# Tying all TensorE work of the RWKV stage to the order of the source, in a one-core hybrid encoder step

## The chip, the cores and the metric

The kernel runs on one core of one Trainium2 chip. The core has five engines with an instruction stream each: TensorE (PE: matmuls and transposes), VectorE (DVE), ScalarE (ACT), GpSimd (POOL) and SyncE (SP, which issues the DMAs). Matmul results land in PSUM, an accumulator memory, from which VectorE and ScalarE read them. An engine takes its instructions in the order in which they stand in its stream; an instruction that needs another engine's result waits for a semaphore, and what stands behind it on its engine waits too. The metric is the device time of one execution in microseconds (us).

## The reference

One layer with three branches over 1,024 prompt positions and 64 sample positions, all from one projection of the normed input:

```python
z = rms_norm(h, prm['norm_g'][l]) @ prm['w_in'][l]
def step(S, inp):                       # branch A, RWKV-7, per head: S is 64 x 64
    r_t, w_t, k_t, v_t, kk_t, a_t = inp
    sa = jnp.einsum('bhij,bhj->bhi', S, -kk_t)
    S = (S * w_t[:, :, None, :] + sa[..., None] * (kk_t * a_t)[:, :, None, :]
         + v_t[..., None] * k_t[:, :, None, :])
    return S, jnp.einsum('bhij,bhj->bhi', S, r_t)
y_b = fox_attention(...)                # branch B: softmax(q.k/8 + c[t] - c[s]), causal
y_c = dsa_attention(...)                # branch C: top 256 keys by an indexer score, then softmax
h = h + gated @ prm['w_out'][l]
y = rms_norm(h, prm['final_g'])
```

## The kernel before

**Stages.** The kernel loads and norms the input, runs the indexer (branch C's scores), then the RWKV stage, then attention (branch B, then branch C) and the output. The projection of the input is split into pieces of 128 columns; `proj` (L154) makes a piece as 8 steps over the 1,024 input dimensions, each of three matmuls (`wb` with `uL`, `wh` with `uH`, `wl` with `uH`; called a k-step here) into a PSUM tile `pproj`. Finished pieces are parked in DRAM. They are *filling*: the pieces stand in a queue, and `pump` deals a few k-steps out behind every step of the other work.

**The RWKV stage** treats the sequence in units of four chunks of 64 positions, 16 units of the prompt and one of the sample. A unit passes through five streams, Python generators that stop at every `yield`: `prep` (`elem`, `chunk_rows`: decays, keys, masked products), `rows` (`value_rows`), `invert` (a 64 x 64 triangular inverse in five levels, the matmuls L1500, L1507 and L1514 in f16), `chain` (the recurrence) and `tail` (norm and gate). `braid` runs one step of them after the other in an interleaved order, with 0.7 k-steps of credit for `pump` behind each, while the top-k search of branch C (`topk`, VectorE and ScalarE only) runs on the side.

A step of the chain for one chunk `c` is: L1588 multiplies the state into PSUM, VectorE adds (L1589, `za`), L1593 multiplies, two VectorE copies make `UV` (L1598), and then, in one step of the source, L1601 makes the state's new part, VectorE turns it into the new state (L1606), and L1610 and L1612 make the output rows:

```python
        ch, ab = G(), self.gring("gd", 1)()
...
            for h in range(2):
                nc.tensor.matmul(ch[hv[h], c * 64:c * 64 + 64], BA[:, h, c, 64 * h:64 * h + 64], UV[:, h, c], start=True, stop=True)
...
            v.scalar_tensor_tensor(self.state, ch[:, c * 64:c * 64 + 64], Pt[:, c, 64:65], sp, op0=OP.mult, op1=OP.add)

            py = ch[:, 256 + c * 64:320 + c * 64]
            for h in range(2):
                nc.tensor.matmul(py[hv[1 - h]], BA[:, h, c, 64 - 64 * h:128 - 64 * h], UV[:, h, c], start=True, stop=False)
```

L1601 and L1610 write different columns of one PSUM tile, `ch` (`ps_gc` in the profile, 512 columns of four bytes), of which there is one buffer. `ps_ga` (the products of `prep` and `rows`) and `ps_tp` (transposes) have one buffer each too, `pproj` and `ps_gb` two.

**What sets the order.** The code is not emitted in the order in which it is written: a scheduler takes the instructions, simulates the engines, and places each where its engine can take it, by priority in the order of the source. Filling has its priority lowered by `LATE`, and `tied` forbids the first TensorE instruction of a filling step to pass TensorE's last instruction of the stream named in `self.now`. So main streams may pass filling and each other, and filling may slip back. One place has been in the order of the source before the change: the eight matmuls of L1442, by `in_order`. `rows_out` (L730) turns keys and values for the caches in three groups through the one `ps_tp` buffer, each group copied out by ScalarE before the next.

Of the kernel before, what the change touches and what calls it, by code (L numbers as in the profile page):

```python
# [85 lines left out]
class K:  # L86
# [77 lines left out]
    def tied(self, gen, engines):  # L164

        ins = self.nc.cur_bb.bb.instructions
        n = len(ins)
        self.tc.cur_priority += LATE
        more = next(gen, self) is not self
        self.tc.cur_priority -= LATE  # L170
        todo = set() if self.free else set(engines)
        for i in ins[n:]:
            if i.engine in todo:
                todo.discard(i.engine)
                for label, behind in self.behind.get(i.engine, {}).items():
                    if self.now and TIE2 and label != self.now:
                        continue
                    self.tc.add_manual_dep(i, behind, mybir.DependencyInfo(
                        mybir.DependencyClass.NoSync, mybir.DependencyReason.DATA), reason="order of issue")
        self.seen = len(ins)  # L180
        return more

    def note(self, label):

        ins = self.nc.cur_bb.bb.instructions
        for i in ins[self.seen:] if label in TIES or not TIES else ():
            self.behind.setdefault(i.engine, {})[label if TIE else 0] = i.name
        self.seen = len(ins)

    def in_order(self, n):  # L190

        last = None
        for i in self.nc.cur_bb.bb.instructions[n:]:
            if i.engine == PE:
                if last is not None:
                    self.tc.add_manual_dep(i, last, mybir.DependencyInfo(
                        mybir.DependencyClass.NoSync, mybir.DependencyReason.DATA), reason="order of issue")
                last = i.name

    def pump(self, n):  # L200

        self.credit = min(self.credit + n, 8)
        while self.credit >= 1 and self.fill:
            self.mark(self.fill[0][0])
            if self.tied(self.fill[0][1], (PE,)):
                self.credit -= 1
            else:
                self.filled.add(self.fill.popleft()[0])
# [1196 lines left out]
    @staticmethod  # L1405
    def dg(t, h):

        return t[64 * h:64 * h + 64, :, 64 * h:64 * h + 64]

    def chunk_rows(self, one, x):  # L1410

        nc = self.nc
        v, g, sc = nc.vector, nc.gpsimd, nc.scalar
        G = self.gring("ga", 1)
        QR, BK, ND = x["QR"], x["BK"], x["ND"]
        dg = self.dg

        BA = one.tile([P, 2, 4, 128], F32, tag="BA", name="BA", bufs=3)  # L1420
        BN = one.tile([P, 2, 4, 64], F32, tag="BN", name="BN", bufs=NBN)
        lo, hi = hv = (slice(0, 64), slice(64, 128))
        p1 = G()
        for c in range(4):
            self.turn(p1[:, c * P:c * P + P], BK[:, c, 0:2].rearrange("p a t -> p (a t)"))
        q1 = p1.rearrange("p (c h d) -> p c h d", h=2, d=64)
        sc.copy(BA[:, 0, :, 0:64], q1[:, :, 0])
        sc.copy(BA[hi, 1, :, 64:128], q1[lo, :, 1])
        sc.copy(BA[lo, 1, :, 64:128], q1[hi, :, 1])
        yield  # L1430
        am = self.con[:, C_AM:C_AM + P].rearrange("p (o x t) -> p o x t", o=1, x=2)
        ps = self.tp()
        nc.tensor.matmul(ps[:, :256], self.ones[:, C_BD - C_M:C_N - C_M], x["rk"], start=True, stop=True)
        x["vb"] = vb = one.tile([P, 4, 64], F32, tag="vb", name="vb", bufs=4)
        v.scalar_tensor_tensor(vb, ps[:, :256].rearrange("p (c t) -> p c t", t=64), 0.5, QR[:, :, 2], op0=OP.mult, op1=OP.mult)
        yield

        pm = G(), self.tp()
        at = len(nc.cur_bb.bb.instructions)
        for c in range(4):  # L1440
            for h in range(2):
                nc.tensor.matmul(pm[h][:, c * P:c * P + P], BK[hv[h], c, h:h + 2].rearrange("p a t -> p (a t)"),  # L1442
                                 QR[hv[h], c, 0:2].rearrange("p a t -> p (a t)"), start=True, stop=True)
        self.in_order(at)
        for h in range(2):
            q = pm[h].rearrange("p (c x t) -> p c x t", x=2, t=64)
            for i, dst in ((1, BN[:, h]), (0, BA[:, h, :, 64 - 64 * h:128 - 64 * h])):
                v.tensor_tensor(dst, q[:, :, i], am[:, :, i].broadcast_to([P, 4, 64]), op=OP.mult)
            g.tensor_scalar(dg(ND[:, 0], h), BN[hv[h], h], 1.0, 0.0, op0=OP.mult, op1=OP.add)
            g.tensor_tensor(dg(ND[:, 1], h), BN[hv[h], h], dg(ND[:, 0], h), op=OP.subtract)  # L1450
            if h == 0:
                yield
        x.update(BA=BA, BN=BN)
        yield
# [330 lines left out]
def program(ctx, tc, I, O):  # L1785
    s = K(ctx, tc, I, O)
# [25 lines left out]
    with ExitStack() as c2:  # L1812
        s.lr = s.pool("lr", ctx=c2, right=True)
        s.zs = s.pool("zs", bufs=1, ctx=c2, right=True)
        s.scp = s.pool("scp", ctx=c2, right=True)
        s.tkp = s.pool("tkp", ctx=c2, right=True)
        s.junk = s.pool("junk", ctx=c2, right=True)
        s.free = True
        s.weave(("idx", s.indexer()), R_IDX[0], R_IDX[1])
        ci.close()  # L1820
        s.rwkv_pools(c2)
        s.need("a0")
        s.free = False
        for nm, w, j in (("a2", s.park_a, 2), ("a3", s.park_a, 3), ("b0", s.park_b, 0),
                         ("b1", s.park_b, 1), ("b2", s.park_b, 2), ("b3", s.park_b, 3)):
            s.fill.append((nm, w(j)))
        for j in range(4):
            s.fill.append((f"c{j}", s.park_c(j)))
        for j in range(4):
            s.fill.append((f"g{j}", s.park_cg(j)))  # L1830
        units = [[(hp, 4 * q + i) for i in range(4)] for hp in range(4) for q in range(4)] + [[(hp, 16) for hp in range(4)]]
        topk = s.topk()
        n = len(units)
        x = [dict(ND=s.ND[u % 2]) for u in range(n)]
        s.weave(("prep0", s.prepare(units[0], x[0])), 10, R_A)
        for u in range(n + 2):
            work = []
            if u >= 2:
                work.append(("tail", s.tail(s.one, x[u - 2]), 3, ()))
            if 1 <= u <= n:  # L1840
                work.append(("chain", s.chain(s.one, units[u - 1], x[u - 1]), NCH, ()))
            if u < n:
                work.append(("invert", s.chunk_invert(s.one, x[u]), 14, ()))
                work.append(("rows", s.value_rows(s.one, x[u], u == n - 1), 2, ()))
            if u + 1 < n:
                if u % 4 == 3 and u < 15:
                    s.need(f"a{u // 4 + 1}")
                work.append(("prep", s.prepare(units[u + 1], x[u + 1]), 10, ()))
            if u < n:
                work.append(("topk", topk, N_TOPK, (DVE, ACT)))  # L1850
            work = [w[:3] for w in work if w[0] != "topk"]
            if u:
                next(s.bias, None)
            s.free = u >= FE
            s.braid(work, R_T if u > n else R_END if len(work) < 3 and u else R_A / 10, ("topk", topk, N_TOPK, (DVE, ACT), work[-1][0] if SIDE < 0 else work[SIDE][0]) if u < n else None)
        for _ in topk:
            pass
        s.need("b0")
        for _ in range(PX):
            s.pump(8)  # L1860
        if FX:
            s.free = False
# [83 lines left out]
```

## Time and profile before

| | |
|---|---|
| three runs, median (lowest to highest) | 1292.87 us (1289.9 to 1293.16) |
| profiled execution, its own time | 1289.49 us |
| its span, first to last instruction | 1286.6 us |
| PE busy, share of the span | 1230.5 us, 96% |
| DVE, ACT, POOL busy | 843.0, 780.3, 671.7 us |
| mean granted TensorE clock | 0.991 of full speed |

The span covers what the instructions take; some 2.9 us of the time lie around it. A matmul's end is modelled, so PE counts as busy up to the end of the last matmul's record, and a wait that starts before that shows shorter than it is. "PEld" is the loading of the stationary operand, which runs beside the matmuls.

### The profile page before, as it was taken

The numbers are of one execution on the slowest core, as the hardware profiler recorded it, in microseconds if no ns is written. First come the engines' busy times: TensorE is split into PE (matmuls) and PEld (weight loads), VectorE is DVE, ScalarE is ACT, GpSimd is POOL, SyncE is SP. The second block draws the span as 40 slices with busy tenths as digits, with TensorE's granted clock in tenths as the row PEclk, the third lists the DMA queues.
The fourth block names the chain that finished last, engine by engine and source line by source line (L and its number), as shares of the span: only waits on it lengthen the run. The fifth ranks groups of instructions, "written<-read, shape, count | busy, mean of one in ns | idle before, by whom it ended". The sixth has DMA issues, their size and how long they took to land.

```text
span 1286.6 us, 29362 instructions
## 1 busy us (share of the span) xinstructions
PE 1230.5 (96%) x10563; PEld 941.8 (73%) x10563; DVE 843.0 (66%) x2487; ACT 780.3 (61%) x1762; POOL 671.7 (52%) x973
## 2 busy tenths in 40 slices
PE   7999999999999999988999989999999889999997
PEld 5777777777777777666777767888887756777764
DVE  7468458888887787998564136556665588666642
ACT  7345357788877888544344456676664587655531
POOL 6333444545545655646454555576666477444311
PEclk9999999999999999989999999999999999999999
DMA  8332421232332443325225389676756476534323
GB/s 231 108 104 68 138 85 52 68 100 71 90 96 73 125 132 105 116 83 170 90 73 162 115 233 268 191 217 201 200 155 183 130 217 171 146 104 114 87 82 95
DMA packets 171699, 168.77 MB, mean 131 GB/s; under 512 B 38641, under 2 KB 146209, under 8 KB 171426
## 3 DMA queue, kind: packets, MB, share of 16 engines
q1 hardware_dynamic: 171554, 166.91, 44.7%
q8 instruction: 83, 1.36, 0.4%
q14 instruction: 62, 0.51, 0.1%
HBM read 106.18 MB, written 62.25 MB: 131 GB/s over the span
## 4 chain that ended last, share of the span: by engine, by line
PE 78%; DVE 9%; DMA 6%; ACT 3%; issue 2%; SPq 1%; POOL 0%; DVEq 0%; POOLq 0%; ACTq 0%
PE pproj L154 37%; PE pproj L1726 7%; PE ps_pv L1005 5%; PE ps_atp L107 4%; PE ps_tp L1726 4%; PE ps_sc L974 2%; PE ps_sc L975 2%; PE ps_gb L1500 2%; PE ps_tp L107 1%; PE ps_gb L1507 1%; ACT junka L613 1%; PE ps_gc L1610 1%; PE ps_gc L1612 1%; PE ps_gc L1601 1%; PE ps_ga L107 1%
## 5 line engine op out<-in xcount | busy, mean ns | idle before, releaser
L154 PE MATMUL pproj<-uH,wh 128*128 128x384 f32 (+4 forms) x1088 | 491.4, 452 | 0.0
L154 PE MATMUL pproj<-uH,wl 128*128 128x384 f32 (+4 forms) x1088 | 361.6, 332 | 0.0
L154 PE MATMUL pproj<-uL,wb 128*128 128x384 bf16 (+4 forms) x1088 | 356.9, 328 | 0.8 <-DVE shift L818 0.5
L154 PEld LDWEIGHTS pproj<-uH,wh 128*128 128x128 f32 (+1 forms) x1088 | 215.8, 198 | 4.8 <-issue 0.7
L154 PEld LDWEIGHTS pproj<-uH,wl 128*128 128x128 f32 (+1 forms) x1088 | 206.5, 190 | 2.0
L154 PEld LDWEIGHTS <-wb 128*128 128x128 bf16 (+1 forms) x1088 | 105.8, 97 | 116.5 <-issue 80.5
L613 ACT ACTIVATE junka<-score,tk_tau 128x1024 f16<-128x1024 f32 (+4 forms) x160 | 149.5, 934 | 33.1 <-DVE junk L607 22.1
L926 POOL TENSOR_SCALAR S<-S,mx 128x128 f32<-128x128 f32 (+8 forms) x136 | 105.6, 780 | 84.1 <-DVE mx L925 62.6
L140 POOL TENSOR_TENSOR wl<-wraw,wh 128x256 fp32r<-128x256 f32 (+1 forms) x184 | 137.8, 780 | 5.8 <-ACT wh L137 4.8
L943 ACT CAST hl<-ps_atp 128x512 fp32r<-128x512 f32 (+3 forms) x184 | 93.6, 515 | 76.8 <-PE ps_atp L107 67.1
L944 DVE TENSOR_TENSOR hl<-ps_atp,hl 128x512 fp32r<-128x512 f32 (+3 forms) x184 | 109.7, 600 | 45.1 <-ACT hl L943 43.4
L921 ACT ACTIVATE S<-S,mx 128x128 f32<-128x128 f32 (+8 forms) x136 | 105.8, 778 | 39.6 <-DVE mx L917 36.1
L142 POOL TENSOR_SCALAR wb<-wraw 128x512 bf16<-128x512 f32 (+1 forms) x92 | 62.9, 701 | 114.3 <-PE pproj L154 66.9
L1005 PE MATMUL ps_pv<-hl,VS 128*128 128x256 f32 (+3 forms) x640 | 111.9, 286 | 7.6 <-ACT hl L943 3.4
L1005 PEld LDWEIGHTS ps_pv<-hl,VS 128*128 128x128 f32 (+1 forms) x640 | 88.7, 173 | 20.7 <-DVE hl L944 4.7
L107 PE MATMUL ps_atp<-ident,S 128*128 128x128 f32 x616 | 101.7, 276 | 1.1 <-DVE hl L944 0.6
L1171 POOL TENSOR_TENSOR cb<-nm,T 128x256 f32<-128x256 bf16 (+2 forms) x80 | 54.3, 685 | 54.5 <-DVE mx L917 52.7
L107 PEld LDWEIGHTS ps_atp<-ident,S 128*128 128x128 f32 x616 | 74.8, 141 | 7.8 <-issue 1.0
L137 ACT CAST wh<-wraw 128x1024 fp32r<-128x1024 f32 (+1 forms) x46 | 47.7, 1037 | 35.9 <-PE pproj L154 35.4
L1726 PE MATMUL pproj<-oh,gh 128*128 128x512 f32 x144 | 67.4, 490 | 0.8 <-ACT oh L1705 0.5
L1726 PE MATMUL pproj<-ol,gb 128*128 128x512 bf16 (+1 forms) x144 | 52.4, 386 | 0.9 <-DVE ol L1706 0.9
L1598 DVE COPY UV<-ps_gd 64x64 f32<-64x64 f32 x136 | 29.9, 220 | 28.7 <-PE ps_gd L1593 26.5
(387 smaller groups left out, 2845.2 us busy)
## 6 DMA issues: line engine op xcount, KB each, us to landing
wraw<-in_w_in_dram SPq DMA_DIRECT2D x45, 512.0 KB
oraw<-in_w_out_dram SPq DMA_DIRECT2D x12, 512.0 KB
out_dram<-rows SPq DMA_DIRECT2D x10, 512.0 KB
x<-in_x_prompt_dram SPq DMA_DIRECT2D x8, 512.0 KB
wt<-a_wa SPq DMA_DIRECT2D x16, 256.0 KB
b_v<-vs SPq DMA_DIRECT2D x8, 512.0 KB
VS<-b_v SPq DMA_DIRECT2D x8, 512.0 KB
d_y<-y SPq DMA_DIRECT2D x64, 64.0 KB
```

The source lines that it names most:

```text
L107: self.nc.tensor.transpose(out, x, self.ident[:n, :n])
L140: nc.gpsimd.tensor_tensor(l[:, k:k + 2, :n], raw[:, k:k + 2, :n], h[:, k:k + 2, :n], op=OP.subtract)
L142: nc.gpsimd.tensor_scalar(b[:, k:k + 4, :n], raw[:, k:k + 4, :n], 1.0, 0.0, op0=OP.mult, op1=OP.add)
L154: self.nc.tensor.matmul(ps[:n, :nt], a[:, k, :n], b[:, k, t0:t0 + nt], start=(k == 0 and i == 0), stop=(k == KD - 1 and i == 2))
L613: nc.scalar.activation(junk[:, :sc.shape[1]], sc, AF.Sign, bias=tf[:, j:j + 1], accum_out=cnt[:, j:j + 1])
L921: nc.scalar.activation(S[:, :kn], S[:, :kn], AF.Exp, bias=mx[:, nm - 1:nm], scale=-1.0, accum_out=mx[:, 6:7])
L926: nc.gpsimd.tensor_scalar(S[:, :kn], S[:, :kn], mx[:, 7:8], 0.5, op0=OP.mult, op1=OP.mult)
L943: nc.scalar.copy(ph[:kr, a:b], ps[:kr, a:b])
L944: nc.vector.tensor_tensor(pl[:kr, a:b], ps[:kr, a:b], ph[:kr, a:b], op=OP.subtract)
L1005: nc.tensor.matmul(pv[0:m, q0:256], VS[:, kb, 0:m], hl[:, x, o:o + w], start=kb == 0 and x == 0, stop=at[-1][0] == last and n == 3)
L1171: nc.gpsimd.tensor_tensor(o, x, y, op=OP.add)
L1726: nc.tensor.matmul(ps[hf][:n, :], parts[m // 4][q][:, m % 4, :n], self.wo[m][q // 2][:, hf * 512:hf * 512 + 512], start=m == 0 and q == 0, ...
```

## The change

`strict` is a new attribute of the kernel. While it is not `None`, `tied` and `note` pass every TensorE instruction that has been emitted since the last call to `in_order`, which ties each to the one before it, and hand the last one's name on to the next call. The RWKV stage sets it from the first `prep` to the end of the loop over units. No instruction is added or taken away.

```diff
@@ tied @@
                     self.tc.add_manual_dep(i, behind, mybir.DependencyInfo(
                         mybir.DependencyClass.NoSync, mybir.DependencyReason.DATA), reason="order of issue")
+        if self.strict is not None:
+            self.strict = self.in_order(n, self.strict or None)
         self.seen = len(ins)
         return more
 
     def note(self, label):
 
         ins = self.nc.cur_bb.bb.instructions
+        if self.strict is not None:
+            self.strict = self.in_order(self.seen, self.strict or None)
...
-    def in_order(self, n):
-
-        last = None
+    strict = None
+
+    def in_order(self, n, last=None):
+
         for i in self.nc.cur_bb.bb.instructions[n:]:
             if i.engine == PE:
...
                 last = i.name
+        return last
@@ chunk_rows @@
-        self.in_order(at)
+        if self.strict is None:
+            self.in_order(at)
@@ program @@
+        s.strict = ""
         s.weave(("prep0", s.prepare(units[0], x[0])), 10, R_A)
         for u in range(n + 2):
...
+        s.strict = None
         for _ in topk:
             pass
```

In the changed kernel the lines of `chain` stand seven further down (L1601 is L1608 there, L1610 is L1617). On TensorE, one step of the chain stands like this before; `ps_gb` rows are the invert stream, `pproj` a k-step of filling, and the brackets name the engine whose semaphore an instruction waits for:

```order
L1601 MATMUL ps_gc<-UV,BA 64x64 [waits DVE_49] x2
L1507 LDWEIGHTS ND_1698
L1507 MATMUL ps_gb<-T_5485,ND_1698 128x64 [waits DVE_49]
...
L154 LDWEIGHTS wb
L154 MATMUL pproj<-uL,wb 128x384
L154 MATMUL pproj<-uH,wh 128x384
L154 MATMUL pproj<-uH,wl 128x384
L1610 MATMUL ps_gc<-UV,BA 64x64 [waits DVE_49]
L1610 MATMUL ps_gc<-UV,BA 64x64
L1612 MATMUL ps_gc<-S,QR 64x64 x2
```

The same step of the same unit on TensorE in the changed kernel:

```order
L154 LDWEIGHTS wb
L154 MATMUL pproj<-uL,wb 128x320
L154 MATMUL pproj<-uH,wh 128x320
L154 MATMUL pproj<-uH,wl 128x320
L1608 MATMUL ps_gc<-UV,BA 64x64 [waits DVE_49] x2
L1617 MATMUL ps_gc<-UV,BA 64x64 [waits DVE_49]
L1617 MATMUL ps_gc<-UV,BA 64x64
L1619 MATMUL ps_gc<-S,QR 64x64 x2
L1507 LDWEIGHTS Y_5668
```

The level of the inverse and the k-step that stood between the two products of the chain now stand elsewhere, and the second product follows the first at once.

The second place is `rows_out` for a piece of keys, on TensorE before; `kT` is the piece, `ps_tp` the one buffer that ScalarE empties between the groups:

```order
L154 MATMUL pproj<-uH,wl 128x320
L107 MATMUL ps_tp<-ident,kT 128x128 x4
L1500 LDWEIGHTS U_6536
L1500 MATMUL ps_gb<-Y_6556,U_6536 64x64 [waits DVE_49]
...
L1601 MATMUL ps_gc<-UV,BA 64x64 [waits DVE_49] x2
L107 MATMUL ps_tp<-ident,kT 128x128 [waits Activation_49]
L107 MATMUL ps_tp<-ident,kT 128x128 x3
```

And the same piece in the changed kernel:

```order
L1595 MATMUL ps_gd<-S,QR 64x64 x2
L107 MATMUL ps_tp<-ident,kT 128x128 x4
L107 MATMUL ps_tp<-ident,kT 128x128 [waits Activation_49]
L107 MATMUL ps_tp<-ident,kT 128x128 x3
L107 MATMUL ps_tp<-ident,kT 64x128 [waits Activation_49]
L154 LDWEIGHTS wb
```

The three groups of transposes, between which other matmuls stood, now stand one behind the other.

## Rows read from the trace of the kernel before

**Rows 1.** The page: span, and busy time by engine
```profile
span 1286.6 us, 29362 instructions
...
PE 1230.5 (96%) x10563; PEld 941.8 (73%) x10563; DVE 843.0 (66%) x2487; ACT 780.3 (61%) x1762; POOL 671.7 (52%) x973
```

**Rows 2.** The page: chain of work that ended last, shares by engine
```profile
PE 78%; DVE 9%; DMA 6%; ACT 3%; issue 2%; SPq 1%; POOL 0%; DVEq 0%; POOLq 0%; ACTq 0%
```

**Rows 3.** Three windows of the RWKV stage: length, busy (x instructions) by engine, clock
```profile
166.00:500.00 334.00, 326.27 (x3969) 247.03 (x3968) 262.27 (x850) 267.07 (x610) 181.22 (x282) 1.00 0.31 93
500.00:605.00 105.00, 93.88 (x1052) 70.35 (x1051) 92.08 (x259) 52.89 (x127) 59.21 (x82) 0.97 0.37 114
605.00:720.00 115.00, 112.82 (x1289) 82.97 (x1290) 58.40 (x180) 45.12 (x114) 56.61 (x88) 1.00 0.31 97
sum 554.00, PE 532.97 PEld 400.34 DVE 412.74 ACT 365.08 POOL 297.04; mean PE 177.66 PEld 133.45 DVE 137.58 ACT 121.69 POOL 99.01
```

**Rows 4.** Waits of PE, 166 to 720 us: total us, times, longest
```profile
PE ps_gc L1610 <- DVE S L1606: 2.3, 6, 0.6
PE ps_ga L107 <- DVE BK L1393: 2.2, 2, 1.1
PE ps_gb L1500 <- DVE Y L1538: 1.9, 6, 0.5
PE ps_gb L1507 <- DVE T L1543: 1.6, 4, 0.6
```

**Rows 5.** Timeline, 301 to 303 us: start, length, instruction
```profile
301.08 0.33 PE L154 MATMUL pproj<-uL,wb 128*128 128x384 bf16 x1
...
301.42 0.34 PE L154 MATMUL pproj<-uH,wl 128*128 128x384 f32 x1
...
301.60 0.34 PE L154 MATMUL pproj<-uL,wb 128*128 128x384 bf16 x1
...
301.95 0.34 PE L154 MATMUL pproj<-uH,wl 128*128 128x384 f32 x1
...
302.21 0.34 PE L1610 MATMUL ps_gc<-UV,BA 128*64 128x64 f32 x4
...
302.60 0.23 PE L1588 MATMUL ps_gd<-S,QR 64*64 64x64 f32 x2
...
302.76 0.34 PE L154 MATMUL pproj<-uL,wb 128*128 128x384 bf16 x1
```

**Rows 6.** Timeline, 419.7 to 421 us
```profile
419.76 0.34 PE L1601 MATMUL ps_gc<-UV,BA 128*64 128x64 f32 x4
...
420.02 0.66 PE L107 MATMUL ps_tp<-ident,kT 128*128 128x128 f32 x4
...
420.61 0.31 PE L1500 MATMUL ps_gb<-Y,U 64*64 64x64 f16 x8
...
420.71 0.59 ACT L730 COPY rows<-ps_tp 128x512 f32<-128x512 f32 x1 [0.43 <-PE ps_tp L107]
```

**Rows 7.** Timeline, 433.9 to 434.9 us; in brackets the idle time before
```profile
433.94 0.34 PE L1601 MATMUL ps_gc<-UV,BA 128*64 128x64 f32 x4
...
434.35 0.28 DVE L1606 SCALAR_TENSOR_TENSOR S<-ps_gc,Pt,sp 128x64 f32<-128x64 f32 x1
...
434.69 0.34 PE L1610 MATMUL ps_gc<-UV,BA 128*64 128x64 f32 x4 [0.41 <-DVE S L1606]
```

**Rows 8.** Line L1606: its instructions, and what DVE sat idle for before them
```profile
L1606 DVE SCALAR_TENSOR_TENSOR S<-ps_gc,Pt,sp x64: 265/280/286, 206.7 to 690.5; 128x64 f32<-128x64 f32 x64
...
L1606 DVE SCALAR_TENSOR_TENSOR s_end<-ps_gc,Pt,sp x4: 283/284/284, 701.1 to 719.1; 128x64 f32<-128x64 f32 x4
...
  PE ps_gc L1601: 20.0, 22
```

**Rows 9.** DVE groups by form, 166 to 720 us: busy, mean ns, idle before
```profile
L607 DVE TENSOR_SCALAR_CACHE_REDUCE junk<-scores,tk_tau 64x576 f16<-64x576 f32 x32 | 25.6, 798 | 4.4 <-ACT junka L613 4.4
```

**Rows 10.** Timeline, 300 to 302 us: the reads of `ps_ga` after L1354
```profile
300.17 0.50 PE L1354 MATMUL ps_ga<-ones,k 128*128 128x2 f32 x4
...
300.53 0.60 PE L107 MATMUL ps_tp<-ident,Yt 128*64 128x128 f32 x4
...
300.70 0.47 ACT L1356 ACTIVATE lw<-ps_ga,par 128x256 f32<-128x256 f32 x1 [0.96 <-PE ps_ga L1354]
...
301.80 0.15 DVE L1359 TENSOR_SCALAR ass<-ps_ga 128x4 f32<-128x4 f32 x1
```

**Rows 11.** Windows around the drop of the clock (the column of 0.72)
```profile
540.00:550.00 10.00, 6.92 (x71) 4.99 (x71) 9.91 (x18) 4.36 (x9) 9.70 (x9) 1.00 0.28 90
550.00:560.00 10.00, 7.90 (x76) 6.13 (x76) 8.74 (x23) 2.79 (x7) 3.30 (x9) 0.72 0.44 151
580.00:595.00 15.00, 11.38 (x135) 8.69 (x133) 14.80 (x38) 8.11 (x23) 12.02 (x20) 1.00 0.68 211
```

**Rows 12.** Timeline of PE, 551 to 553 us
```profile
551.52 0.50 PE L154 MATMUL pproj<-uL,wb 128*128 128x384 bf16 x1
...
552.46 0.54 PE L154 MATMUL pproj<-uL,wb 128*128 128x384 bf16 x1
```

## The prediction, made before the changed kernel had run

> **What bounds the kernel now.** I read the page first. TensorE is busy for 1230.5 of 1286.6 us [rows 1], and 78% of the chain of work that ended last lies on it [rows 2]: what TensorE loses anywhere, the kernel loses, unless it was waiting there already. Next the windows of the stage that the change reorders, from 166 us (the first product of `prep`) to 720 us (the last product of the chain). TensorE is busy for 532.97 of 554.00 us there, so all its idle time is 21.0 us [rows 3]: 7.7 us up to 500, 11.1 us from 500 to 605, where DVE is busy for 92.08 of 105 us and is nearly the bound itself, and 2.2 us after. The list of waits splits this into many small ones: six of L1610 for the state, two of L107 for `BK`, six of L1500 and four of L1507 for the levels of the inverse [rows 4]. So the most that any order of this stage could win is 21 us, 1.6% of the time; there is no such limit on what one can lose.
>
> **What the change moves.** The changed order holds the same instructions. From the first product of `prep` to the first score of attention I count 5,547 matmuls in both orders, 1,917 of them filling; ahead of that stretch and behind it TensorE's orders are the same. Inside it, filling stood in 276 runs and now stands in 455, nearly always one k-step at a time. Four terms follow.
>
> *Changes of hands.* From a k-step's last matmul to the next k-step it is 0.18 us (301.42 to 301.60); a recurrence product follows a k-step's last matmul after 0.26 us (301.95 to 302.21), and a k-step follows a recurrence product after 0.16 us (302.60 to 302.76) [rows 5]. 179 more runs mean 179 x (0.26 + 0.16) = 75 us; against it stand 213 fewer borders between two k-steps (38 us) and 276 fewer between two recurrence groups (44 us at 0.16). That is -7 us at the outside and nothing to the accuracy of these borders; I take 0. The matmuls themselves cost what they did.
>
> *The state in the chain.* This is the term that decides. L1601 and L1610 are one step of the source, and in the changed order L1610 stands right behind L1601 in all 68 steps of the chain (16 units of four chunks and the sample's four), where before this was so in three, and elsewhere a level of the inverse, k-steps or transposes stood between. L1610 waits for DVE, and by the trace for L1606, which reads the new state's product out of the same PSUM tile. One of the three shows the price: L1601 starts at 433.94, L1606 runs from 434.35 to 434.63, L1610 starts at 434.69 [rows 7], 0.75 us after L1601, though DVE was free. Where something else follows L1601, it starts 0.26 us behind (419.76 to 420.02) [rows 6]. So each new neighbour costs 0.49 us, and 65 of them 32 us. That is for a free DVE. In 22 of its 68 runs L1606 found DVE idle and waiting for it [rows 8]; in the other 46 something was ahead in DVE's queue. Bounds for that: nothing at all below, and above a whole top-k count of 0.80 us [rows 9] each time, 37 us. A DVE instruction of the first window takes 262.27 / 850 = 0.31 us on average [rows 3]; it is nearest to the usual case, and 46 x 0.31 = 14 us is what I take. The term: 46 us, from 32 to 69. Queued behind L1610 on TensorE is all its work, so nothing covers the wait.
>
> Why L1610 waits at all, when it writes other columns than L1606 reads, no row says. [...]
>
> *Transposes through one buffer.* `rows_out` runs seven times inside the tied stretch, and its three groups now stand together, so that two of them wait for ScalarE's copy: 14 waits. A group starts at 420.02, the next matmul follows at 420.61, but the copy of `ps_tp` ends at 420.71 + 0.59 = 421.30 [rows 6], and with the 0.06 us that L1610 took after L1606's end [rows 7] the next group could start at 421.36: 0.75 us each, 10.5 us. The copy is not sooner than its input, so this is the lower end; another ScalarE instruction of 0.47 us [rows 10] ahead of it each time would make 17 us.
>
> *`ps_ga`.* `prep`'s first product (L1354) and `rows`' transposes (L107 of `QR`) use the same single buffer, and now stand one k-step apart. L1354 started at 300.17, its last reader L1359 ended at 301.80 + 0.15 = 301.95 [rows 10]; between the two there will be L1354's own 0.36 us (to 300.53) and a k-step's 0.52, so the transposes wait 1.78 + 0.06 - 0.88 = 0.96 us as it was here, or 0.33 us if L1359 follows L1356 (300.70 + 0.47) at once. With 16 such pairs 5 to 15 us; I take the middle, 10 us.
>
> *What the old waits give back.* Between the inverse's products there is now a k-step or a chain product almost everywhere, so the waits of L1500 and L1507 should largely go; those from 500 to 605 us come from DVE, which isn't relieved. I take half of the 21.0 us, 10.5 us; the bounds are all and none.
>
> The sum is 46 + 10.5 + 10 - 10.5 = 56 us. On the profiled execution's own 1289.49 us that is 1345.5 us; that execution was 3.4 us under the median of the three runs shown, 1292.87, which makes 1349 us, and I say 1348 because waits that come at the same moment count once. Low end: 32 + 10.5 + 5 - 21 = 26.5 us, 1319 us. High end: 69 + 17 + 15 - 0 = 101 us, 1394 us; all terms at their worst together are unlikely, and the range ends at 1386 us.
>
> **The rivals.** *DVE's queue in full (chance 0.11).* If L1606 stands behind a top-k count in all 46 cases, and `ps_ga`'s reader too, the time is 1394 us. For it: DVE is busy for 79% up to 500 us and 88% from 500 to 605 [rows 3]. Against: while TensorE waits, DVE catches up.
>
> *The clock (0.05).* At 551 us the granted clock fell to half: a k-step took 0.94 us (551.52 to 552.46) [rows 12] instead of 0.52, after ten microseconds in which TensorE was busy for 6.92 [rows 11]. The clock column of 550 to 560 is 0.72, so 5.6 of the ten ran at half speed; a k-step loses 0.42 of its 0.94 us there, so such a stretch costs some 2.5 us. If the new waits bring on one in each of the 17 units, the time is 43 us longer than forecast, 1391 us. Against: from 580 to 595 us TensorE was busy for 11.38 of 15 us and kept the full clock [rows 11], and the forecast leaves it busy for 533 of 610, 87%. [...]
>
> *Faster (0.03).* If L1606 were done in time everywhere, the fixed order would show only its good side: all 21.0 us of waits gone, 1272 us. It decides where more than 0.49 us of other work stands between L1601 and L1610; the order shows none. The same comes about if the old waits were caused by the scheduler's misjudged times, and the new ones are shorter than a free DVE needs, which [rows 7] speaks against.
>
> *No change that shows (0.03), within 0.3%, which is about what a measurement of this kernel can tell from none.* The losses would have to be covered because DVE is the true bound. That holds from 500 to 605 us at most, and by its share of the stage's time 13 of the 68 chain steps lie there: 6 of the 32 us.
>
> My forecast has 0.78. The range of 1319 to 1386 us holds it and the nearer half of the first two rivals. Slower by over 0.3%: 0.78 + 0.11 + 0.05 = 0.94; within 0.3%: 0.03; faster: 0.03.
>
> **What would show it.** In the list of TensorE's waits, `ps_gc` L1617 (L1610 before) for the state of L1613 (L1606) should come first, some 68 times, with 20 to 40 us shown (part of each wait lies under the modelled end of L1608). L107 should wait some 14 times for the copy of `rows` (L736 there) and some 15 times for `ass` (L1365). L1608 to L1617 should take 0.75 us or more from start to start. TensorE's idle time between the same two products should grow from 21 to 60 or 90 us, and attention should take as long as before. I am wrong if L1617 waits for less than 0.2 us a time, if waits of the inverse take the place of those that I count as gone, or if the clock column of the stage falls under 0.95.

## The result and the profile after

| | before | after |
|---|---|---|
| median of four runs (lowest to highest) | 1293.01 us (1289.9 to 1293.91) | 1411.37 us (1408.96 to 1413.29) |
| profiled execution, its own time | 1289.5 us | 1413.2 us |

The ratio is 1.0928, 95% interval 1.0901 to 1.0955: slower by 118 us, where 56 were forecast. The time lies outside the range. The two profiled executions differ by 123.7 us, and the accounts below go by these.

The page of the changed kernel (first row span, then busy time, then the granted clock in 40 slices, then the chain that ended last):

```profile
span 1411.4 us, 29349 instructions
...
PE 1281.9 (91%) x10563; PEld 968.2 (69%) x10563; DVE 844.4 (60%) x2487; ACT 786.4 (56%) x1762; POOL 668.4 (47%) x973
...
PEclk9999989999899999989999999999999989999999
...
PE 70%; DVE 12%; ACT 6%; DMA 6%; issue 3%; POOL 2%; SPq 1%; DVEq 0%; POOLq 0%; ACTq 0%
```

DVE, ACT and POOL are busy for as long as before [rows 1], TensorE for 51 us more, though it has the same 10,563 matmuls. So TensorE did not only wait: its matmuls took longer, or started further apart.

Windows of the reordered stage, with the columns of [rows 3]; the fourth is the whole of it, from the first product of `prep` (146.9 us, not the 166 that the prediction names; before it was 146.1) to the first score of attention (869.8, before 750.1), and the last row is the whole stage before the change:

```profile
166.00:500.00 334.00, 293.27 (x3252) 215.29 (x3250) 219.14 (x712) 227.87 (x509) 140.00 (x224) 0.95 0.23 70
500.00:605.00 105.00, 89.16 (x980) 64.51 (x980) 69.03 (x224) 63.54 (x144) 46.86 (x76) 0.93 0.34 105
605.00:720.00 115.00, 91.59 (x975) 66.35 (x976) 78.91 (x204) 40.11 (x99) 55.15 (x78) 0.93 0.28 88
...
146.00:870.00 724.00, 628.73 (x6626) 459.12 (x6625) 422.22 (x1312) 391.82 (x894) 321.07 (x499) 0.95 0.29 88
...
146.00:750.00 604.00, 582.31 (x6620) 437.14 (x6618) 423.56 (x1312) 386.23 (x894) 327.86 (x499) 0.99 0.34 104
```

TensorE is busy for 628.73 of 724 us, 87%, the share that was forecast. The column to look at is the clock: 1.00, 0.97 and 1.00 before, 0.95, 0.93 and 0.93 now.

TensorE's waits in that stage (total, times, longest):

```profile
PE ps_gc L1617 <- DVE S L1613: 48.8, 64, 2.2
PE ps_tp L107 <- ACT rows L736: 15.4, 14, 2.2
PE ps_ga L107 <- DVE ass L1365: 10.0, 16, 2.0
PE ps_gc L1608 <- DVE UV L1605: 3.4, 1, 3.4
PE ps_gb L1514 <- DVE T L1550: 2.9, 6, 1.2
...
PE ps_gc L1617 <- DVE s_end L1613: 1.9, 4, 0.5
```

The three waits that were forecast are the three largest, in the places and as often as forecast: 68, 14 and 16 times. Together they are 76.1 us of the 95.2 us that TensorE stands idle between the two products named (21.4 before).

One of the 68 at work, on TensorE and then on VectorE:

```profile
299.85 0.34 PE L1608 MATMUL ps_gc<-UV,BA 128*64 128x64 f32 x4
302.04 0.34 PE L1617 MATMUL ps_gc<-UV,BA 128*64 128x64 f32 x4 [1.86 <-DVE S L1613]
```

```profile
300.13 0.41 DVE L1455 TENSOR_TENSOR BA<-ps_ga,con 128x256 f32<-128x256 f32 x1
300.46 0.15 DVE L823 COPY shift<-pproj 128x1 f32<-128x1 f32 x1
300.52 0.41 DVE L1455 TENSOR_TENSOR BN<-ps_tp,con 128x256 f32<-128x256 f32 x1
300.86 0.41 DVE L1455 TENSOR_TENSOR BA<-ps_tp,con 128x256 f32<-128x256 f32 x1
301.19 0.15 DVE L824 COPY shift<-pproj 128x1 f32<-128x1 f32 x1
...
301.38 0.41 DVE L1545 TENSOR_TENSOR Y<-ps_gb,con 128x256 f16<-128x256 f32 x1
301.72 0.27 DVE L1613 SCALAR_TENSOR_TENSOR S<-ps_gc,Pt,sp 128x64 f32<-128x64 f32 x1
```

L1613 needs what L1608 wrote by 300.2, but six instructions of other streams (and two more, left out here) stand ahead of it in VectorE's queue. L1617 starts 0.05 us after L1613's end, 2.19 us after L1608. And now the clock (windows of two microseconds, the same columns):

```profile
301.00:303.00 2.00, 0.96 (x19) 0.78 (x19) 1.50 (x9) 1.63 (x5) 1.52 (x3) 1.00 0.71 282
303.00:305.00 2.00, 2.00 (x12) 1.29 (x10) 0.85 (x4) 1.24 (x2) 1.35 (x2) 0.67 0.03 8
305.00:307.00 2.00, 2.00 (x15) 1.57 (x15) 1.06 (x4) 1.11 (x3) 0.00 (x0) 0.50 0.00 0
```

TensorE was idle for half of 301 to 303; from 303.7 on it runs at half of the full clock (0.50 from 305 to 307), while it is busy all the time. The granted clock falls 15 times in the stage and is at half speed for 71.7 us in all by the clock records (before: twice, 6.8 us). This fall is like the others: in the five microseconds ahead of each of the 15, TensorE stood idle for 1.3 to 3.1 us, where five microseconds of the stage hold 0.7 us of idle time on average. Other stretches with as much idle time kept the full clock (from 665 to 670 TensorE was idle for 2.04 us, and the clock column is 1.00 there and up to 675).

One thing more changed, which no list of waits shows. Before, the chain's last product (L1612) and the next chunk's first (L1588) mostly started within 0.01 us of each other, so that the two took little longer than one (the fourth row of these, at 302.60, and the k-step behind it, at 302.76, stand in [rows 5]):

```profile
302.48 0.27 PE L1612 MATMUL ps_gc<-S,QR 64*64 64x64 f32 x2
302.49 0.27 PE L1588 MATMUL ps_gd<-S,QR 64*64 64x64 f32 x2
302.59 0.22 PE L1612 MATMUL ps_gc<-S,QR 64*64 64x64 f32 x2
```

In the changed kernel a k-step follows the last product (L1619) in 50 of 68 steps, and L1619 alone takes as long, 0.26 us to the next start, as the two together before, 0.28 us:

```profile
224.38 0.33 PE L1619 MATMUL ps_gc<-S,QR 64*64 64x64 f32 x4
224.64 0.34 PE L154 MATMUL pproj<-uL,wb 128*128 128x384 bf16 x1
```

### The profile page after: what moved, and what is told of

Same layout as the page of the kernel before. It is cut to its first block, busy times and chain, and to the rows that moved or that the text cites. A ratio compares the mean times of both kernels' runs of the same rounds, so it can differ in the third digit from the quotient of the medians.

```text
span 1411.4 us, 29349 instructions
## 1 busy us (share of the span) xinstructions
PE 1281.9 (91%) x10563; PEld 968.2 (69%) x10563; DVE 844.4 (60%) x2487; ACT 786.4 (56%) x1762; POOL 668.4 (47%) x973
## 4 chain that ended last, share of the span: by engine, by line
PE 70%; DVE 12%; ACT 6%; DMA 6%; issue 3%; POOL 2%; SPq 1%; DVEq 0%; POOLq 0%; ACTq 0%
PE pproj L154 32%; PE pproj L1733 7%; PE ps_pv L1011 4%; PE ps_atp L107 4%; PE ps_tp L1733 4%; ACT junka L619 2%; PE ps_sc L980 2%; PE ps_sc L981 2%; PE ps_gb L1507 2%; DVE junk L613 1%; PE ps_gc L1617 1%; PE ps_tp L107 1%; DVE S L1613 1%; PE ps_gc L1619 1%; PE ps_gd L1595 1%
## 5 line engine op out<-in xcount | busy, mean ns | idle before, releaser
L154 PE MATMUL pproj<-uH,wh 128*128 128x384 f32 (+4 forms) x1088 | 503.7, 463 | 0.0
L154 PE MATMUL pproj<-uH,wl 128*128 128x384 f32 (+4 forms) x1088 | 366.1, 336 | 0.0
L154 PE MATMUL pproj<-uL,wb 128*128 128x384 bf16 (+4 forms) x1088 | 363.3, 334 | 0.5 <-DVE shift L824 0.5
L154 PEld LDWEIGHTS pproj<-uH,wh 128*128 128x128 f32 (+1 forms) x1088 | 220.5, 203 | 5.1
L154 PEld LDWEIGHTS pproj<-uH,wl 128*128 128x128 f32 (+1 forms) x1088 | 212.2, 195 | 1.4
L142 POOL TENSOR_SCALAR wb<-wraw 128x512 bf16<-128x512 f32 (+1 forms) x92 | 59.4, 664 | 120.3 <-issue 63.1
L1617 PE MATMUL ps_gc<-UV,BA 128*64 128x64 f32 x272 | 23.2, 250 | 50.6 <-DVE S L1613 48.8
L1456 POOL TENSOR_SCALAR ND<-BN 64x256 f16<-64x256 f32 x34 | 13.7, 402 | 113.3 <-DVE BN L1455 112.1
```

The lines of the kernel that those rows point to most:

```text
L142: nc.gpsimd.tensor_scalar(b[:, k:k + 4, :n], raw[:, k:k + 4, :n], 1.0, 0.0, op0=OP.mult, op1=OP.add)
L154: self.nc.tensor.matmul(ps[:n, :nt], a[:, k, :n], b[:, k, t0:t0 + nt], start=(k == 0 and i == 0), stop=(k == KD - 1 and i == 2))
```

## The experiments

All are compared with before. *Stage* is the time from the first product of `prep` (L1316 of before) to the first score of attention, *idle* the sum of TensorE's shown idle times in it, *half* the time at which the granted clock was 0.5 in it; all come from the profiled executions. *Left over* is the stage less before's 604.0, less the idle time above 21.4, less 0.45 us for each us of half above 6.8; 0.45 is (0.94 - 0.52) / 0.94, from [rows 12] and the prediction's full-speed k-step. Each ratio is against runs of the kernel before that were taken with it, whose medians are 1290.3 to 1293.0 us. The executions of one kernel differ in their clock: e1's profiled one, the slowest of its four (1353.7 us), was granted 0.971 and the other three 0.980 to 0.982, and in e3, e5, e6 and e7 too the profiled one had the lowest clock. *Half* is therefore on the high side in these rows.

| kernel | median us | ratio, 95% | stage | idle | half | left over | behind the stage |
|---|---|---|---|---|---|---|---|
| before | 1293.0 | | 604.0 | 21.4 | 6.8 | 0 | 536.5 |
| after | 1411.4 | 1.0928 [1.0901, 1.0955] | 723.0 | 95.2 | 71.7 | 16.0 | 541.6 |
| e1_banks | 1347.5 | 1.0457 [1.0431, 1.0483] | 665.3 | 56.2 | 54.6 | 5.0 | 540.3 |
| e2_before_banks | 1304.2 | 1.0114 [1.0096, 1.0132] | 615.4 | 28.4 | 17.1 | -0.2 | 540.3 |
| e3_dummy | 1398.6 | 1.0847 [1.0822, 1.0873] | 711.5 | 51.8 | 47.8 | more work | 540.0 |
| e4_banks_rows | 1339.5 | 1.0387 [1.0367, 1.0406] | 654.2 | 50.4 | 37.5 | 7.4 | 535.6 |
| e5_main_only | 1343.7 | 1.0398 [1.0372, 1.0423] | 654.3 | 57.7 | 47.8 | -4.5 | 542.6 |
| e6_banks_rows_tp | 1312.3 | 1.0158 [1.0142, 1.0174] | 628.4 | 35.3 | 17.1 | 5.9 | 535.2 |
| e7_late_py | 1358.3 | 1.0507 [1.0485, 1.0528] | 667.8 | 57.9 | 54.6 | 5.8 | 541.1 |
| e8_before_late_py | 1300.2 | 1.0070 [1.0056, 1.0083] | 609.8 | 21.0 | 13.7 | 3.1 | 541.5 |
| e9_before_rows | 1292.8 | 1.0009 [0.9995, 1.0022] | 607.0 | 24.1 | 6.8 | 0.3 | 534.3 |
| e10_main_banks | 1315.4 | 1.0178 [1.0154, 1.0202] | 627.9 | 36.1 | 27.3 | 0.0 | 536.5 |

**e1, the state's product in a bank of its own, in the changed kernel.** It trades places with L1600's product; no product is added.

```diff
-            pa, pb = [ab[:, 256 * i + c * 64:256 * i + c * 64 + 64] for i in range(2)]
+            pa, pb, st = ab[:, c * 64:c * 64 + 64], ch[:, c * 64:c * 64 + 64], ab[:, 256 + c * 64:320 + c * 64]
...
-                nc.tensor.matmul(ch[hv[h], c * 64:c * 64 + 64], BA[:, h, c, 64 * h:64 * h + 64], ...)
+                nc.tensor.matmul(st[hv[h]], BA[:, h, c, 64 * h:64 * h + 64], ...)
...
-            v.scalar_tensor_tensor(self.state, ch[:, c * 64:c * 64 + 64], Pt[:, c, 64:65], sp, ...)
+            v.scalar_tensor_tensor(self.state, st, Pt[:, c, 64:65], sp, ...)
```

> The changed kernel, with the state's product of the chain (L1608) moved into the PSUM bank of ps_gd and L1600's product moved out of it into ps_gc; the order on TensorE stays that of the source and nothing is left out. L1617 then writes a bank that VectorE's state instruction L1613 doesn't read. Theory A, the wait for the bank costs 0.82 us in each of 68 chain steps (56 us) and the idle time that it makes is what brings the clock down (65 us more at half speed than before, worth some 29 us): 1411 - 56 - 25 = 1330 us, waits of L1617 for L1613 gone, half-speed time back to under 25 us. Theory B, the wait costs 56 us but the clock falls for the other waits or for the order itself: 1355 us and some 60 us at half speed still. Theory C, L1617 waits for the state for another reason than the bank: 1411 us, waits as before.

It ran 64 us faster than after. The time lies between the theories A and B. The half-speed time of the profiled execution, 54.6 us, is nearer to B's 60; by their mean clocks the other three had some 25 to 30 us less of it over the whole kernel. So with this wait gone a part of the half-speed time goes, and a part stays. Theory C is out. Who waited for L1613, in e1:

```profile
  ACT sp L1597: 33.0, 24
  ACT Yt L1623: 2.5, 2
  PEld ps_gd L1595: 1.0, 2
  PEld L1507: 0.9, 4
  PE ps_gd L1595: 0.4, 1
```

L1617 no longer waits at all, though it still follows L1608 at once: it starts 0.17 us after it, where it was 1.09 us on average in after. So the wait came from the shared bank and not from the data (`ch` and `ab` are a PSUM tile of 512 columns each, and a bank here is such a tile; the runs do not tell a wait set by the tile from one set by its place in PSUM, nor why there is one when the columns differ). The traces have 68 waits with one bank and none with two. TensorE's largest waits in e1:

```profile
PE ps_tp L107 <- ACT rows L736: 16.6, 14, 2.2
PE ps_ga L107 <- DVE ass L1365: 14.1, 16, 2.3
PE ps_gb L1514 <- DVE T L1550: 6.8, 11, 1.4
PE ps_gb L1507 <- DVE Y L1545: 5.5, 8, 1.5
```

They are all longer than in after, where the second pair had 2.9 and 2.0 us: of the 50.7 us taken away 11.7 came back elsewhere (56.2 us idle, not 44.5). VectorE and ScalarE have the same work to do in 58 us less.

**e2, the same exchange in the kernel before**, with the same diff.

> The kernel before, with the same exchange of the two products between the PSUM banks, free order. Theory A: only the 2.8 us of waits of L1610 for the state can go, so 1288 to 1293 us, the same within the measurement; L1610 follows L1601 directly more often. Theory C: no change in where L1610 stands or waits. Against a gain: the first product of a unit's chain now shares its bank with the state product, and za's reads with it, which could cost up to 0.5 us in each of 17 units, 1301 us.

It is 1.1% slower, outside what was expected. The exchange has a price of its own in the free order; if it has the same in the fixed one, which no run shows, e1 undercounts what the state's wait costs. Of the 11.4 us in its stage 7 are idle time, most of it at the inverse: L1500 waits 5.7 us for L1538's `Y` (1.9 before [rows 4]), and the half-speed time grows by 10 us.

**e3, work in place of the wait.** Two products of 128 x 128 that nobody reads stand between L1608 and L1617 of the changed kernel, in another bank.

```diff
+            for _ in range(2):
+                nc.tensor.matmul(ab[:, 256:384], self.ident, self.ones[:, C_BD - C_M:C_N - C_M], start=True, stop=True)
             py = ch[:, 256 + c * 64:320 + c * 64]
```

> The changed kernel, with two 128x128 matmuls of constants between L1608 and L1617 in each of the 68 chain steps, into columns of ps_gd that nothing reads any more; the results stay the reference's. They take some 0.4 us, in a wait of 0.8 us that stays. Theory A, idle time in the chain's wait brings the clock down: the wait hides the matmuls, TensorE is active through it, half-speed time falls from 72 us in the stage to under 25 and the time to about 1411 - 22 = 1389 us. Theory B, the clock falls for other reasons: 1411 us and 72 us at half speed. If the wait doesn't hide them: 1411 + 68 x 0.4 = 1438 us.

The page's busy row, and from the list of waits the one for the state (L1619 is L1617 of after):

```profile
PE 1313.7 (94%) x10835; PEld 999.2 (71%) x10835; DVE 838.6 (60%) x2487; ACT 785.6 (56%) x1762; POOL 665.8 (48%) x973
```

```profile
PE ps_gc L1619 <- DVE S L1613: 12.8, 19, 1.6
```

With 136 products more the kernel is 13 us *faster* than after. They took nothing from VectorE's work, and they lie in the wait: the shown wait for the state fell from 50.7 us to 12.8, TensorE is busy for 32 us more. What the kernel gained is mostly half-speed time, 47.8 us instead of 71.7: of the 11.5 us by which its stage is shorter the matmuls at half speed account for 9 to 11. It is not one lucky profile, since the mean granted clock is 0.974 to 0.982 in its four executions and 0.965 to 0.973 in those of after. Were the waits the whole loss, filling them could at best have changed nothing. The result lies between the theories: the clock fell in part for this wait, but the forecast 25 us at half speed and 1389 us were not reached.

**e4, e1 with the middle group of `rows_out` through a projection bank.**

```diff
-            ps = self.tp()
+            ps = self.proj_bank() if g == 1 else self.tp()
```

> As the first of these, and the middle one of the three groups of transposes that turn keys and values into rows goes through a projection bank instead of ps_tp, so that two groups are in flight. Theory: of the 15.4 us in which L107 waited for ScalarE's copy of the rows half or more goes, 8 to 12 us under the first run: 1320 us if that comes to 1330.

The time fell by 8 us, as expected, and the wait for `rows` from 16.6 to 4.3 us. In the stage the idle time fell by only 5.8 us, and 4.7 us were won behind it. That the half-speed time fell with it (54.6 to 37.5) is not shown: over all their executions the two kernels have about the same mean clock (0.971 to 0.982 and 0.976 to 0.983).

**e6, e4 with the transposes of `QR` in `ps_tp`**, so that they no longer follow L1354's readers through the one `ps_ga`.

```diff
-        p2 = G()
+        p2 = self.tp()
```

> The changed kernel with the state's product in another bank and the middle group of the rows through a projection bank (as the fourth run, 1339 us), and the transposes of QR (L107) through ps_tp in place of ps_ga, so that they no longer wait for the readers of the low-rank products. Theory: the 15.8 us of waits for `ass` go, and with them a part of the 37.5 us at half speed (by the runs so far 0.9 us at half speed for each us of idle time, 0.45 us lost in each): 1339 - 16 - 6 = 1317 us. If other waits take their place on ps_tp: 1335 us or more.

27 us faster than e4, 5 us better than expected: the wait for `ass` goes from 15.8 to 2.4 us and the half-speed time from 37.5 to 17.1. With the three forecast waits gone or cut down, the fixed order is 1.6% slower than before, not 9.3%. The largest waits that are left are the inverse's, 14.1 of 35.3 us:

```profile
PE ps_gb L1514 <- DVE T L1550: 7.3, 9, 2.4
PE ps_gb L1507 <- DVE Y L1545: 6.8, 9, 1.1
```

**e5, the main streams tied to one another, filling only as before**: `tied` no longer passes its instructions on.

```diff
-        if self.strict is not None:
-            self.strict = self.in_order(n, self.strict or None)
         self.seen = len(ins)
         return more
```

> One part of the change alone: the main streams are tied to the order of the source on TensorE, the filling is tied only as before, so the scheduler may put it between. Its order holds 31 of 68 places where L1615 (L1610 before) still follows L1606 (L1601) at once; the three groups of the cache rows, and the transposes behind the low-rank products, have other matmuls between them again. Theory A, what costs is tying the filling, which is then not there where a main stream waits: of the 118 us the 25 us of the 31 waits stay and some 10 us of lower clock, 1325 us. Theory B, the order among the main streams is what costs: over 1370 us.

The time fell between the two. In 30 of 68 steps of the trace L1615 (L1617 of after) still stands right behind the state's product, in 32 only filling stands between; it waits 40 times for the state, and four times more (1.8 us) for the sample's:

```profile
PE ps_gc L1615 <- DVE S L1611: 29.8, 40, 2.2
```

So more than half of the loss goes when filling may move, since it then stands between the two products in half of the steps. Theory A had the count right and the price too low: the waits for the state come to 32 us instead of 25, and the 47.8 us at half speed, 41 more than before, are worth some 18 us instead of 10.

**e7, in the changed kernel, the output products one step of the chain later in the source** (L1617 and L1619 become a function that is called at the head of the next chunk's step), which separates the two products without a change of banks.

```diff
-            py = ch[:, 256 + c * 64:320 + c * 64]
...
+            if late:
+                rows_of(*late)
             za, sp = [one.tile([P, 64], F32, tag=n, name=n) for n in ("za", "sp")]
...
+            late = c, S
```

> The changed kernel, with the two output products of a chain step (L1617 and L1619, here L1588 and L1590) written one step of the source later, just ahead of the next chunk's first product; banks as before, everything tied, nothing left out. A k-step or more then stands between the state's product and them. Theory A, the neighbourhood costs, not the bank as such: the 50.7 us of waits for the state go and the time is 1411 - 64 = 1347 us, as with the other bank, or up to 14 us less, since the exchange of banks made the kernel before 14 us slower. Theory B, the wait only moves to the next instruction: 1400 us or more.

53 us faster than after, 11 us above theory A and far from B: no wait for the state is left, and a second way of taking the same neighbours apart gives nearly what e1 gave. Here the last product of a chain step stands ahead of the next chunk's first again, and mostly starts within 0.02 us of its neighbour, as before.

**e8, the same in the kernel before.**

> The kernel before, free order, with the output products of a chain step written one step later in the source. Theory A: the 2.8 us of waits of L1610 go, other waits come and go with the scheduler's new order: 1284 to 1296 us, the same.

0.7% slower than before and above the expected range, with as much idle time. Moving the products does not help where the scheduler already kept them apart.

**e9, e4's edit of `rows_out` alone, in the kernel before.**

> The kernel before, in its own order, with one edit: the middle of the three groups of transposes in rows_out goes through a projection bank instead of the one ps_tp buffer. In the ordered kernel this edit, on top of the exchanged banks, was worth 8 us (1347.5 to 1339.5), some 5 of them behind the RWKV stage (540 to 536 us). If that part has nothing to do with the fixed order, it shows here too: 1286 to 1290 us, with the rest behind the stage at some 532 us instead of 536.5. Rival: in the free order the scheduler already puts other matmuls between the groups, and the projection bank is taken from filling, so that a k-step waits for it: 1292 to 1296 us.

No change; the time is in the rival's range, and the expected gain did not come: behind the stage it is 2 us shorter, in the stage 3 us longer. The free order had already put other work between the groups.

**e10, e5 and e1's banks together.**

> Only the main streams are tied to one another, filling is tied only as before the change, and the state's product has a bank of its own, so that nothing stands on the state's read. If the loss is waits of TensorE plus the half-speed time that they bring, it should fall with the idle time: the main-only kernel had 1343.7 us with 32 us of waits for the state; without these some 25 us of idle time are left, and with 1.4 us lost for each it ends at 1298 to 1310 us. Rival: an order of the main streams among themselves costs by itself (short waits hidden under the modelled ends, for T, Y, rows and ass), so that taking out the state's wait only moves it: 1325 us or more. On both theories the idle time and the half-speed time in the stage should lie on the line of the ten kernels so far, 0.9 us at half speed for each us of idle time.

1315.4 us, 5 above the first theory's range and 10 under the rival. Its stage is 23.9 us longer than before's: 14.7 us of idle time and 20.5 us of half speed at 0.45, 9.2 us, make up all of it. So the account by waits and their clock closes, and in this kernel the order of the main streams costs nothing beside these. What was wrong in the expectation is the amount of waiting left, 36 us instead of 25, and the line for the half-speed time, 27.3 us where it gave 20. The waits moved:

```profile
PE ps_gb L1512 <- DVE T L1548: 10.7, 15, 3.2
PE ps_tp L107 <- ACT rows L734: 6.4, 7, 1.8
PE ps_ga L1320 <- ACT UV L1484: 5.1, 5, 1.7
```

No version beats the kernel before.

## Why the prediction was right in direction and wrong in size

Its direction and the place of each forecast wait were right. The sum of 56 us was less than half of what came. Two steps failed: the clock, for which it had no term, and the changes of hands, which it put at nothing. One of its own signs of being wrong came true: the clock column of the stage fell to 0.93. Term by term, the span of the profiled executions being 124.8 us longer (1286.6 and 1411.4):

**The state in the chain** (46 us forecast): shown 48.8 + 1.9 = 50.7 us. L1617 starts 1.09 us after the first L1608 on average, 0.75 us in the quickest tenth and 1.85 us or more in the slowest; before, without shown idle time, it was 0.31 us to whatever came next, so that this is 68 x 0.78 = 53 us, nearly all of it shown. With 0.75 us in all 68 steps it would be 30 us (32 forecast), and VectorE's queue makes the other 23 (14 forecast). L1613 found VectorE idle in 28 of 68 cases (22 of 68 before [rows 8]). The price for a free VectorE was right, the queue was taken too short.

**Transposes through one buffer** (10.5): 15.4 us in 14 waits, within the bounds of 10.5 to 17. The forecast was for a free ScalarE; it stood idle for the transposes ahead of only 11 of the 30 copies.

**`ps_ga`** (10): 10.0 us in 16 waits. That it is so exact is luck: 10 was the middle of 5 to 15.

**What the old waits give back** (-10.5): 95.2 - 50.7 - 15.4 - 10.0 leaves 19.1 us of other waits, against 21.4 before: 2.3 us given back, not 10.5. The inverse's largest waits are still there (`T` 2.9, `Y` 2.0 us), and single long ones are new, as the 3.4 us of L1608 for `UV`.

**Changes of hands** (0) is a step that failed. Taken from start to start, without the shown idle times and at full clock, the matmuls of the stage took 21 us more than before. A matmul into `pproj` went from 175 to 182 ns (1,917 of them: 14 us more), one into `ps_ga` from 77 to 61 ns (832: 13 us less), into `ps_gc` from 54 to 70 ns (816: 13 us more), into `ps_tp` from 134 to 145 (333: 4 us more), and the others 3 us more. These are not parts of the forecast waits under modelled ends. Of the 13 us of `ps_gc`, 11.6 lie behind L1619 (15 ns before, 57 after), 1.4 behind L1608 and none behind L1617; of the 4 us of `ps_tp`, 3.5 lie behind the masked products (L1448) and 0.4 behind the transposes. What the prediction missed is that neighbours can overlap: it credited 0.16 us for every border between two recurrence groups that went, but between L1612 and L1588 such a border had been 0.01 us, and behind L1619 there is now one of 0.15 us to a k-step. In e7, where the last product stands ahead of the next chunk's first again, `ps_gc` is back at 53 ns.

**The clock** (no term; a rival with a chance of 0.05) is the other step that failed. It was dismissed because TensorE had kept the full clock at 11.38 busy of 15 us [rows 11] and the forecast left it busy for 87%. It was busy for 87%, and it fell 15 times. The mean share did not show this: from 580 to 595 us the idle time happened to lie in a way that did no harm, and that was one case. At half clock the matmuls of the stage took 67.2 us from start to start, without shown idle times, where at this kernel's own full-clock averages by tile they would have taken 39.6: 27.6 us, some 25 more than before (by the 0.45 of the table, 29). What the kernel would win without the falls may be less: over 54 executions of the eleven kernels other than before, each compared with its own kernel's mean, a us more at half speed (from the mean granted clock) goes with 0.27 us more of time, which makes 18 us. The rival's own price of 43 us for 17 falls was too high, but by e3 it was right that the new waits bring falls on.

**Attention as long as before**: 541.6 us against 536.5, 5 us more, with 25.7 us at half clock there instead of 11.9. Why, no run shows; it is so in some kernels with the order of before as well (e2, e8).

The sum of what was measured is 50.7 + 15.4 + 10.0 - 2.3 + 21 + 25 + 5 = 125 us: all of the difference, since the idle times and the start-to-start times make up the stage between them.

The theory after the result was that waits cause the half-speed time and each us of it loses nearly half; the rival, that the fixed order costs by itself, through the borders between streams. Both hold, the rival for the smaller part. By start-to-start times at full clock the borders cost 21 us in the changed kernel and 7 to 9 us in e1, e4, e6 and e7, in which filling is tied too; with filling free and the source of the chain unchanged (e2, e5, e9, e10) they cost -4 to 0.4 us. The waits and their clock are the rest. Over the twelve profiled executions the half-speed time goes with the idle time, from 21 us and 7 to 14 at one end to 95 us and 72 at the other: above before's values 0.9 us for each us of idle time in the changed kernel, and 0.7 to 1.5 in the others that stand idle longer (e9 apart, with 2.7 us more idle and no more half speed). One us of shown wait thus goes with 1 + 0.9 x 0.45 = 1.4 us in the changed kernel, and 1.3 to 1.7 in the others; with 0.27 in place of 0.45 it is 1.2 to 1.4. That idle time brings the clock down, and not both something else, rests on e3, where work in its place raised the clock in every execution, and on the idle time ahead of each of the 15 falls. How many falls a given idle time brings is not settled: the four executions of the changed kernel, all of one order, had 76 to 99 us at half speed over the whole kernel by their mean clocks.

What stays open: why e2's exchange costs the kernel before 14 us (1.1%) rather than nothing, what decides in one execution or another whether the clock falls, and why attention took longer.

## What to carry to other kernels

Before tying an order by hand, list which neighbours on the tied engine share a PSUM bank with another engine's read between them: the pair of L1608 and L1617 took 0.75 us from start to start in the quickest tenth and 1.85 us or more in the slowest, by what VectorE's queue held, where it had been 0.31 us to whatever came next, and giving such neighbours banks of their own at three places took 99 of 118 us of the loss away here (e6), though it did not make the fixed order better than the free one. List also which short products start together with a neighbour, as L1612 and L1588 did: here a border that overlapped was nearly free (0.01 us), and the new neighbour made it cost 0.15 us. In this kernel, in which TensorE was busy for 96% of the span before, a us of short, frequent waits went with 1.2 to 1.7 us of time, because the clock fell with them (to 0.95, 0.93 and 0.93 in the three windows). Whether it stays up is to be read from the clock column, stage by stage, and not argued from the mean busy share.

## What the runs showed that I had not expected

TensorE busy for 87% of a stage ran at 0.95 of the full clock, where before, at 582.31 of 604 us (96%), it ran at 0.99. Products that nobody reads, put into its waits, made the kernel 13 us faster (e3). And exchanging two PSUM columns with no more work (e2) made the free order 1.1% slower, although TensorE's idle time grew by only 7 us: the other part was half speed, 17.1 us against 6.8, and 4 us behind the stage.
